# A decoder trunk on one core: decays' differences on VectorE, attention heads in token order, four weight loads moved behind the last operands

## The chip, the cores and the metric

The kernel runs on 1 core of a Trainium2 chip. The metric is device time in microseconds of one execution; the time before is the median of three runs. Engines: PE is TensorE (matrix products), DVE is VectorE, ACT is ScalarE, POOL is GpSimd, SP is SyncE, which here issues nearly all transfers. Each engine works through its own queue in the order in which the program put it there, and an instruction that waits holds everything behind it in that queue.

## The reference

Sequence 512, model width 1024, float32. Two layers, each a mixer and a feed-forward part with a residual; an RMS norm stands ahead of each and at the end.

```python
for i in range(2):
    h = rmsnorm(x, mix_norm_w[i])
    x = x + (dilated_attention_mixer(h) if i == 0 else ssd_mixer(h))
    x = x + conv_ffn(rmsnorm(x, ffn_norm_w[i]))
return rmsnorm(x, final_norm_w)
```

The attention has 8 heads of 128, each with three dilations (1, 4, 16) that a softmax joins. The second mixer is a chunked state-space scan; its part that the change touches is the decay matrix of each head and chunk of 128 tokens, with `a_cs` the running sum of the decay rates:

```python
seg  = a_cs[:, :, :, None] - a_cs[:, :, None, :]
lmat = exp(where(causal, seg, -inf))
y_diag = einsum("bcijgr,bcjgrp->bcigrp", cb[..., None] * lmat, xdt)
```

It has 32 heads of 64 in 8 groups, and each group is closed by a gated RMS norm of its own.

## The kernel before

Activations lie as 8 tiles of 128 features by 512 tokens. Every float32 operand of a large product is split in a high and a low part (`xh`/`xl` for activations, `hi`/`lo` for weights), and `mm3` makes a product of three matmuls of 512 columns. A weight unit of 128x1024 comes by a transfer into `raw` (4 buffers), a cast on ACT (`hi`, L125) and a difference on DVE (`lo`, L126; `load_unit`). Results land in PSUM banks: `mm_bank` gives three in a ring, so a product can start only when the engine that reads the bank's last result but two has done so. That reader is a DVE instruction: `us` (L694, in `ssm_tile`: `usxs`, `usb`, `usc`, `usz`) for a projection of the state-space mixer, the sum into the residual `xr` (L872) for its output rows `wso`.

*Order.* PE's order is written out by hand (`manual_schedule`). That of DVE, ACT, POOL and SP is set by the scheduler that records the program, from its own estimates; `queued(name)` and `issue_after` hold an instruction behind a named one in that order.

*Attention.* `attend(h)` works in a token order by residue of 4. Its last step adds the bank `po` (rows in blocks, then residue) to a copy of `pg` into `o`, and splits `o` into `oh`, `ol`. After the last head the output product `wo` is added into `xr` (L551), where the tokens are brought back into natural order by a strided access on both SBUF operands; `prep` then splits `xr[m]` into `xh[m]`, `xl[m]` (L200, L201) and sums its squares.

*Norm and projection.* `norm_and_project` runs the first three projections behind a norm while the last `xh`/`xl` come in: k = 0 to 6 of two of them, then k = 7. The mean goes PE (`ss`), DVE (`ms`), POOL (`rcol`), PE (`rb`), ACT (`rbc`). It is used twice: ahead of the first feed-forward (units `u0_0` to `u0_2`) and ahead of the state-space mixer (`xs00`, `wdt`, `b0`).

*State-space mixer.* `project_group(g)` makes x0, b, c, x1, z0, z1 of group g, `scan_group(g)` the scan. While PE projects group g + 1, the scan of group g goes: `decays` (four tiles `lm` and two `ee`, read back from `rows` by transfers; differences and exponentials on ACT), `by_token` (`xdt` on DVE from the bank `px`, `xdd` on POOL, `btok` on ACT), `cb` (DVE), `states` (PE `pst`), `lm` times `cb` (POOL), `products` (PE `py`, `pf`), `outputs` (DVE `yt`, ACT squares `gsq`), the sum of the two squares (DVE L840), the mean and the norm. The differences of the next group (L768, 16 instructions of 128x128) are held behind the second square of the group before; `latest["square"]` names it.

Of the kernel before, what the change touches and what calls it, by code (L numbers as in the profile page):

```python
# [22 lines left out]
DIL = 4  # L23
# [28 lines left out]
def trunk(ctx: ExitStack, tc: tile.TileContext, A, out):  # L52
    nc = tc.nc
    V, SC, G, T = nc.vector, nc.scalar, nc.gpsimd, nc.tensor
# [12 lines left out]
    def mm_bank(name):  # L67
        return ps.tile([P, 512], F32, tag="mm", name=name, bufs=3)
# [7 lines left out]
    def t2(name, tag, bufs, pool=k2, dtype=F32):  # L76
        return pool.tile([P, 512], dtype, tag=tag, name=name, bufs=bufs)
# [32 lines left out]
    def col(c):  # L110
        return par[:, c : c + 1]
# [21 lines left out]
    def long_product(dst, w, x, first, last):  # L133
        T.matmul(in_turns(dst), w, in_turns(x), start=first, stop=last)  # L134

    def mm3(dst, hi, lo, at, rh, rl, first, last):
        w_h = hi[:, at * P : (at + 1) * P]
        w_l = lo[:, at * P : (at + 1) * P]
        long_product(dst, w_h, rh, first, False)
        long_product(dst, w_h, rl, False, False)  # L140
        long_product(dst, w_l, rh, False, last)

    early = {}

    def project(src, name, low=V):
        if name in early:
            return early.pop(name)
        hi, lo = load_unit(src, name, low=low)
        t = mm_bank(name)
        for k in range(KD):  # L150
            mm3(t, hi, lo, k, xh[k], xl[k], k == 0, k == KD - 1)
        return t

    def norm_and_project(ssum, srcs):

        units = [(load_steps() if name == "wdt" else load_unit(src, name), mm_bank(name), name) for src, name in srcs]

        def part(i, ks):
            (hi, lo), t, name = units[i]
            for k in ks:  # L160
                if name == "wdt":
                    steps_products(t, hi, k)
                else:
                    mm3(t, hi, lo, k, xh[k], xl[k], k == 0, k == KD - 1)

        with tc.manual_schedule(engines={mybir.EngineType.PE}):
            part(0, range(KD - 1))
            part(1, range(KD - 1))
            part(0, [KD - 1])
            part(1, [KD - 1])  # L170
            inv_rms(ssum, D, rcol)
            part(2, range(5))
            p = along_free(rcol, "rb")
            SC.copy(rbc, p)
            part(2, range(5, KD))
        for _, t, name in units:
            early[name] = t

    def load_steps():

        raw = wr.tile([P, 1024], F32, tag="raw", name="raw_wdt")[:, : KD * NSH]
        both = wh.tile([P, 1088], F32R, tag="hi", name="hi_wdt")[:, : 2 * KD * NSH]
        dma(raw, A["wdt"])
        raw3, both4 = raw.rearrange("p (k h) -> p k h", k=KD), both.rearrange("p (k b h) -> p k b h", k=KD, b=2)
        SC.copy(both4[:, :, 0], raw3)
        V.tensor_tensor(both4[:, :, 1], raw3, both4[:, :, 0].bitcast(F32), op=ALU.subtract)
        return both, None

    def steps_products(dst, both, k):
        w = both[:, k * 2 * NSH : (k + 1) * 2 * NSH]  # L190
        long_product(dst[0 : 2 * NSH, :], w, xh[k], k == 0, False)
        long_product(dst[0 : 2 * NSH, :], w, xl[k], False, k == KD - 1)


    def prep(k, src, c_w, ssum):
        split(k, src, c_w)
        square(k, src, ssum)

    def split(k, src, c_w):
        SC.activation(xh[k], src, AF.Copy, scale=col(c_w + k))  # L200
        V.scalar_tensor_tensor(  # L201
            xl[k], src, col(c_w + k), xh[k].bitcast(F32), op0=ALU.mult, op1=ALU.subtract
        )

    def square(k, src, ssum, add=G):
        if k == 0:
# [94 lines left out]
    ssum = t2("ssum", "ssum", 2)  # L301
# [45 lines left out]
    def in_blocks(ap):  # L347

        return ap.rearrange("p (n r l) -> p r n l", n=4, r=DIL)

    def by_residue(ap):
        return ap.rearrange("p (r n l) -> p r n l", n=4, r=DIL)

# [28 lines left out]
    scale = HD ** -0.5  # L382
    oh, ol = [], []

    def attend(h):
# [89 lines left out]
        po, pg = aux_bank(f"po{h}"), aux_bank(f"pg{h}")  # L475
# [5 lines left out]
        values(2)  # L481
        values(3)
        o = t2(f"o{h}", "o", 1, s3)
        SC.copy(in_blocks(o), by_residue(pg))
        V.tensor_tensor(o, o, po, op=ALU.add)
        o_h, o_l = high_low(f"o{h}")
        SC.copy(o_h, o)
        V.tensor_tensor(o_l, o, o_h.bitcast(F32), op=ALU.subtract)
# [49 lines left out]
    xr = [lp.tile([P, S], F32, tag=f"xr{k}", name=f"xr{k}") for k in range(KD)]  # L538
    for k in range(KD):
        dma(xr[k], A["xt"][k])  # L540

    def natural(ap):
        return ap.rearrange("p (n l r) -> p n r l", n=4, r=DIL)

    ssum = t2("ssum1", "ssum", 2)
    for m in range(KD):
        if m not in wo_held:
            wo_first(m)
        hi, lo, p = wo_held[m]
        mm3(p, hi, lo, NH - 1, oh[-1], ol[-1], False, True)  # L550
        V.tensor_tensor(  # L551
            natural(xr[m]), natural(xr[m]), p.rearrange("p (n r l) -> p n r l", n=4, r=DIL),
            op=ALU.add
        )
        prep(m, xr[m], C_FFN, ssum)


# [45 lines left out]
            with tc.manual_schedule(engines={mybir.EngineType.PE}):  # L603
                down(f"wd{layer}{part}", load, range(KD), lambda c: (gh[c], gl[c]), cn, add, late=True)

    def up_first(layer):
        return [(A["wup"][layer * 44 + i], f"u{layer}_{i}") for i in range(3)]

    norm_and_project(ssum, up_first(0))
    ssum_a = t2("ssum2", "ssum", 2)  # L610
    ffn(0, lambda m: prep(m, xr[m], C_MIX + KD, ssum_a))
    norm_and_project(ssum_a, [(A["win"][0], "xs00"), (A["wdt"], "wdt"), (A["win"][2], "b0")])


    def b3(ap, n):
# [8 lines left out]
    dtt, adt, acs, dec, cdec = (cst(n) for n in ("dtt", "adt", "acs", "dec", "cdec"))  # L624
# [60 lines left out]
    latest = {}  # L685
# [33 lines left out]
    def scan_group(g, d, ys):  # L719
# [34 lines left out]
        def decays():  # L754

            for x in range(2):
                ee.append(t2("ee", "ee", 2, lp))
                for hp in range(2):
                    h, half = heads[x].start + hp, slice(hp * 64, (hp + 1) * 64)
                    t = t2("lm", "lm", 4, lp)  # L760
                    dma(t, rows[h : h + 1, :].to_broadcast([P, S]))
                    dma(ee[x][half, P:512], rows[h : h + 1, P:512].to_broadcast([64, S - P]))
                    lm.append(t)
            with queued("square"):
                for i, t in enumerate(lm):
                    for c in range(NCH):
                        cs, at = slice(c * P, (c + 1) * P), c * NSH + heads[0].start + i
                        SC.activation(t[:, cs], t[:, cs], AF.Relu, bias=acs[:, at : at + 1], scale=-1.0)  # L768
            with queued("gate"):
                for x in range(2):  # L770
                    SC.activation(ee[x][:, P:512], ee[x][:, P:512], AF.Exp)
                for t in lm:
                    latest["decay"] = SC.activation(t, t, AF.Exp, scale=-1.0)

        def products(x):

# [22 lines left out]
        def outputs(x, py, pf):  # L799
            yt = t2("yt", "yt", 2, lp)  # L800
            V.tensor_tensor(ee[x][:, P:512], ee[x][:, P:512], pf[:, P:512], op=ALU.mult)
            V.scalar_tensor_tensor(
                yt, xs[x], col(C_DSK + 2 * g + x), py, op0=ALU.mult, op1=ALU.add
            )
            V.tensor_tensor(yt[:, P:512], yt[:, P:512], ee[x][:, P:512], op=ALU.add)
            V.tensor_tensor(yt, yt, d[f"z{x}"], op=ALU.mult)
            sq = t2("gsq", "sq", 2)
            latest["square"] = SC.activation(sq, yt, AF.Square)
            return yt, sq

        decays()
# [10 lines left out]
        for c in range(NCH):  # L822
            cs = slice(c * P, (c + 1) * P)
# [13 lines left out]
        banks = [f() for f in carried]  # L837
        yield
        (y0, sq0), (y1, sq1) = (outputs(x, *b) for x, b in enumerate(banks))
        V.tensor_tensor(sq0, sq0, sq1, op=ALU.add)  # L840
        yield
        rg = sm.tile([P, 4], F32, tag="rg", name="rg")
        latest["mean"] = inv_rms(sq0, 2 * P, rg, bank=side_bank)
# [325 lines left out]
```

## Time and profile before

| | |
|---|---|
| median of the runs | 1653.52 us (1652.71 to 1653.53, 3 runs) |
| profiled execution | 1652.15 us, span 1650.4 us |
| mean granted clock of TensorE | 0.999 |
| busy: PE, DVE, ACT, POOL | 1633.2, 1039.9, 695.3, 456.9 us |
| stretches | attention to about 515 us, feed-forward to 858, state-space mixer to 1285, feed-forward to the end |

Busy time of PE counts overlapping matmuls once, so what matters is where it waits, and what ends the wait. In the chain that ended last, PE has 86%, DVE 6%, ACT 4%.

### The profile page before, as it was taken

The page shows a single profiled execution, that of the slowest core. Times are in us where ns is not written, and L with a number is a line of the kernel's source. Part 1 is how long each engine was busy: PE and PEld are TensorE (multiplying, and loading weights), DVE is VectorE, ACT ScalarE, POOL GpSimd, SP SyncE. Part 2 cuts the span into 40 slices and gives each one's busy share as a digit, 9 for nine tenths or more (in the row PEclk, how much of TensorE's full clock was granted, in tenths as well). Part 3 has the DMA queues.
Part 4 walks back from the last instruction along what each step waited for, and adds up shares of the span by engine and source line. Part 5 has one row for each costly group of instructions (what it writes and reads, how often), then busy time and mean ns, then how long its engine had stood idle before and what let it go on. Part 6 is the DMA issues. An engine that isn't in the chain of part 4 may idle for free.

```text
span 1650.4 us, 21521 instructions
## 1 busy us (share of the span) xinstructions
PE 1633.2 (99%) x8236; PEld 1396.8 (85%) x8236; DVE 1039.9 (63%) x1672; ACT 695.3 (42%) x1115; POOL 456.9 (28%) x294
## 2 busy tenths in 40 slices
PE   9999999999999999999999999999999999999998
PEld 8888888888888888888888887888878888888888
DVE  6366555366648755755656677766777684574565
ACT  5233332333345433432445745555562552343345
POOL 0443443044503310220232222332331341121022
PEclk9999999999999999999999999999999999999999
DMA  7322222222224323323233333233432332332323
GB/s 255 103 79 75 80 88 89 90 77 90 77 80 138 101 87 106 102 90 115 74 109 121 105 114 104 74 122 112 138 102 74 101 104 89 115 102 90 104 76 128
DMA packets 54391, 168.32 MB, mean 102 GB/s; under 512 B 6353, under 2 KB 9809, under 8 KB 54289
## 3 DMA queue, kind: packets, MB, share of 16 engines
q1 hardware_dynamic: 53456, 166.15, 30.4%
q8 instruction: 65, 1.06, 0.3%
q10 hardware_dynamic: 832, 0.79, 0.1%
q14 instruction: 38, 0.30, 0.1%
HBM read 164.76 MB, written 2.16 MB: 101 GB/s over the span
## 4 chain that ended last, share of the span: by engine, by line
PE 86%; DVE 6%; ACT 4%; issue 2%; DMA 2%; POOL 0%; DVEq 0%; POOLq 0%; ACTq 0%; SPq 0%
PE u L134 28%; PE qk L134 15%; PE wd L134 12%; PE v L134 8%; PE wso L134 3%; PE xs L134 3%; PE z L134 3%; PE b L134 2%; PE c L134 2%; PE wo L134 2%; PE wz L134 1%; ACT lm L768 1%; DVE axs L561 1%; PE pp L448 1%; PE pg L461 1%
## 5 line engine op out<-in xcount | busy, mean ns | idle before, releaser
L134 PE MATMUL u<-xh,lo_u 128*128 128x512 f32 x704 | 269.0, 382 | 0.0
L134 PE MATMUL u<-xh,hi_u 128*128 128x512 f32 x704 | 268.7, 382 | 0.0
L134 PE MATMUL u<-xl,hi_u 128*128 128x512 f32 x704 | 266.4, 378 | 0.3 <-DVE xl L201 0.3
L583 POOL TENSOR_TENSOR au<-au,au 128x512 f32<-128x512 f32 x43 | 56.9, 1322 | 423.8 <-DVE au L561 397.3
L561 DVE SCALAR_TENSOR_TENSOR au<-usu,par,au 128x510 f32<-128x510 f32 (+1 forms) x176 | 160.8, 918 | 6.2 <-ACT au L559 1.3
L363 POOL TENSOR_TENSOR rotqk<-rotqk,sr 32x512 f32<-32x512 f32 x48 | 91.9, 1915 | 256.3 <-DVE rotqk L362 208.9
L125 ACT CAST hi_u<-raw_u 128x1024 fp32r<-128x1024 f32 x88 | 91.2, 1044 | 169.9 <-PE u L134 97.1
L134 PEld LDWEIGHTS u<-xl,hi_u 128*128 128x128 f32 x704 | 131.7, 187 | 25.2 <-DVE xl L201 0.7
L134 PEld LDWEIGHTS u<-xh,lo_u 128*128 128x128 f32 x704 | 131.7, 187 | 23.9
L134 PEld LDWEIGHTS u<-xh,hi_u 128*128 128x128 f32 x704 | 131.7, 187 | 21.5
L134 PE MATMUL qk<-xh,hi_qk 128*128 128x512 f32 x384 | 148.8, 388 | 0.0
L134 PE MATMUL qk<-xh,lo_qk 128*128 128x512 f32 x384 | 147.1, 383 | 0.0
L134 PE MATMUL qk<-xl,hi_qk 128*128 128x512 f32 x384 | 147.0, 383 | 0.0
L126 DVE TENSOR_TENSOR lo_u<-raw_u,hi_u 128x1024 fp32r<-128x1024 f32 x88 | 111.1, 1268 | 25.9 <-ACT hi_u L125 25.9
L576 DVE TENSOR_TENSOR usu<-u,rbc 128x512 f32<-128x512 f32 x88 | 60.5, 690 | 103.1 <-PE u L134 93.8
L596 DVE TENSOR_TENSOR xr<-xr,wd 128x512 f32<-128x512 f32 x40 | 27.2, 687 | 117.2 <-PE wd L134 117.2
L125 ACT CAST hi_qk<-raw_qk 128x1024 fp32r<-128x1024 f32 x48 | 50.2, 1046 | 99.6 <-PE v L134 49.8
L125 ACT CAST hi_wd<-raw_wd 128x1024 fp32r<-128x1024 f32 (+1 forms) x56 | 52.4, 952 | 90.2 <-PE wd L134 55.9
L359 DVE TENSOR_TENSOR qk<-qk,cr 128x512 f32<-128x512 f32 x48 | 33.0, 687 | 90.5 <-PE qk L134 90.3
L134 PEld LDWEIGHTS qk<-xh,lo_qk 128*128 128x128 f32 x384 | 71.9, 187 | 13.0
L134 PEld LDWEIGHTS qk<-xl,hi_qk 128*128 128x128 f32 x384 | 72.0, 187 | 12.4
L134 PEld LDWEIGHTS qk<-xh,hi_qk 128*128 128x128 f32 x384 | 71.9, 187 | 11.7
(641 smaller groups left out, 3909.1 us busy)
## 6 DMA issues: line engine op xcount, KB each, us to landing
raw_u<-in_wup SPq DMA_DIRECT2D x88, 512.0 KB, 3.2
raw_qk<-in_wqk SPq DMA_DIRECT2D x48, 512.0 KB, 3.2
raw_wd<-in_wdn SPq DMA_DIRECT2D x32, 512.0 KB, 3.2
raw_wd<-in_wdn SPq DMA_DIRECT2D x24, 384.0 KB, 3.0
raw_xs<-in_win SPq DMA_DIRECT2D x16, 512.0 KB, 3.2
raw_z<-in_win SPq DMA_DIRECT2D x16, 512.0 KB, 4.0
lm<-rows SPq DMA_DIRECT2D x32, 256.0 KB, 5.5
raw_wso<-in_wso SPq DMA_DIRECT2D x16, 512.0 KB, 3.3
```

The lines of the kernel that those rows point to most:

```text
L125: SC.copy(hi[:, s], raw[:, s])
L126: low.tensor_tensor(lo[:, s], raw[:, s], hi.bitcast(F32)[:, s], op=ALU.subtract)
L134: T.matmul(in_turns(dst), w, in_turns(x), start=first, stop=last)
L359: V.tensor_tensor(at(t), of(p), of(cr), op=ALU.mult)
L363: G.tensor_tensor(rot[R, :], rot[R, :], sr[R, :], op=ALU.mult)
L448: T.transpose(pp[:, b * P : (b + 1) * P], pr[:, b * P : (b + 1) * P], ident)
L461: T.matmul(pg[:, ii], vt[g, half][i][:, es], pts[i][:, (g + 1) * P : (g + 2) * P], start=g == 1, stop=g == 2,)
L561: V.scalar_tensor_tensor(dst[:, j:], src[:, : S - j], col(c_w + taps - 1 - j), dst[:, j:], op0=ALU.mult, op1=ALU.add,)
L576: V.tensor_tensor(us, p, rbc, op=ALU.mult)
L583: by.tensor_tensor(ab[1], ab[0], ab[1], op=ALU.mult)
L596: V.tensor_tensor(xr[m], xr[m], p, op=ALU.add)
L768: SC.activation(t[:, cs], t[:, cs], AF.Relu, bias=acs[:, at : at + 1], scale=-1.0)
```

## The change

Four edits. The 16 differences of each group are computed on DVE (subtract and a minimum with 0 in place of a Relu of the negated difference; the exponential loses its sign), and they are held behind the sum of the two squares instead of the second square. `o` is written in natural token order: ACT's copy and DVE's sum carry the strides, and the sums into `xr` become plain. `norm_and_project` takes two further units (`u0_3`, `u0_4`; `c0`, `xs01`) whose loads are issued behind the last `xh` and `xl`; `project` then finds them in `loaded`. `square` of the outputs is otherwise unchanged.

```diff
+    loaded = {}
     early = {}
     def project(src, name, low=V):
         if name in early:
             return early.pop(name)
-        hi, lo = load_unit(src, name, low=low)
+        hi, lo = loaded.pop(name) if name in loaded else load_unit(src, name, low=low)
...
-    def norm_and_project(ssum, srcs):
+    def norm_and_project(ssum, srcs, more):
...
+        with tc.issue_after(last_split[0].ins), tc.issue_after(last_split[1].ins):
+            for src, name in more:
+                loaded[name] = load_unit(src, name)
...
-        SC.copy(in_blocks(o), by_residue(pg))
-        V.tensor_tensor(o, o, po, op=ALU.add)
+        SC.copy(o.rearrange("p (n l r) -> p r n l", n=4, r=DIL), by_residue(pg))
+        V.tensor_tensor(natural(o), natural(o), po.rearrange("p (n r l) -> p n r l", n=4, r=DIL), op=ALU.add)
...
-        V.tensor_tensor(
-            natural(xr[m]), natural(xr[m]), p.rearrange("p (n r l) -> p n r l", n=4, r=DIL),
-            op=ALU.add
-        )
+        V.tensor_tensor(xr[m], xr[m], p, op=ALU.add)
...
-    norm_and_project(ssum, up_first(0))
+    norm_and_project(ssum, ups(0, range(3)), ups(0, (3, 4)))
...
-    norm_and_project(ssum_a, [(A["win"][0], "xs00"), (A["wdt"], "wdt"), (A["win"][2], "b0")])
+    norm_and_project(ssum_a, [(A["win"][0], "xs00"), (A["wdt"], "wdt"), (A["win"][2], "b0")], [(A["win"][3], "c0"), (A["win"][1], "xs01")])
...
-                        SC.activation(t[:, cs], t[:, cs], AF.Relu, bias=acs[:, at : at + 1], scale=-1.0)
+                        V.tensor_scalar(t[:, cs], t[:, cs], acs[:, at : at + 1], 0.0, op0=ALU.subtract, op1=ALU.min)
...
-                    latest["decay"] = SC.activation(t, t, AF.Exp, scale=-1.0)
+                    latest["decay"] = SC.activation(t, t, AF.Exp)
...
-            latest["square"] = SC.activation(sq, yt, AF.Square)
+            SC.activation(sq, yt, AF.Square)
...
-        V.tensor_tensor(sq0, sq0, sq1, op=ALU.add)
+        latest["square"] = V.tensor_tensor(sq0, sq0, sq1, op=ALU.add)
```

What stands in the queues: PE's order and that of SP's transfers are the same before and after. On DVE, at the end of group 2, before (`usz` and `usxs` read the banks of the last z and of the x projected ahead, `xr` those of two `wso`):

```order
L806 TENSOR_TENSOR yt<-yt,usz_7725 128x512
L694 TENSOR_TENSOR usz_8195<-z_8170,rbc 128x512
L806 TENSOR_TENSOR yt<-yt,usz_7815 128x512
L126 TENSOR_TENSOR lo_c_8408<-raw_c_8406,hi_c_8407 128x1024
L840 TENSOR_TENSOR gsq<-gsq 128x512
L694 TENSOR_TENSOR usxs_8265<-xs_8240,rbc 128x512
L872 TENSOR_TENSOR xr_4046<-xr_4046,wso_8285 128x512
L126 TENSOR_TENSOR lo_xs_8486<-raw_xs_8484,hi_xs_8485 128x1024
```

and after:

```order
L813 TENSOR_TENSOR yt<-yt,usz_7725 128x512
L701 TENSOR_TENSOR usz_8195<-z_8170,rbc 128x512
L813 TENSOR_TENSOR yt<-yt,usz_7815 128x512
L126 TENSOR_TENSOR lo_c_8408<-raw_c_8406,hi_c_8407 128x1024
L847 TENSOR_TENSOR gsq<-gsq 128x512
L775 TENSOR_SCALAR lm<-lm,acs 128x128 x16
L701 TENSOR_TENSOR usxs_8265<-xs_8240,rbc 128x512
L126 TENSOR_TENSOR lo_xs_8486<-raw_xs_8484,hi_xs_8485 128x1024
L879 TENSOR_TENSOR xr_4046<-xr_4046,wso_8285 128x512
```

The sixteen differences (L775) stand ahead of `usxs`; `usz` stays ahead of them. At the end of group 3 on DVE, before:

```order
L806 TENSOR_TENSOR yt<-yt,usz_8195 128x512
L840 TENSOR_TENSOR gsq<-gsq 128x512
L694 TENSOR_TENSOR usz_8643<-z_8618,rbc 128x512
L126 TENSOR_TENSOR lo_c_8856<-raw_c_8854,hi_c_8855 128x1024
L694 TENSOR_TENSOR usxs_8713<-xs_8688,rbc 128x512
```

and after:

```order
L813 TENSOR_TENSOR yt<-yt,usz_8195 128x512
L847 TENSOR_TENSOR gsq<-gsq 128x512
L775 TENSOR_SCALAR lm<-lm,acs 128x128 x16
L701 TENSOR_TENSOR usz_8643<-z_8618,rbc 128x512
L126 TENSOR_TENSOR lo_c_8856<-raw_c_8854,hi_c_8855 128x1024
L701 TENSOR_TENSOR usxs_8713<-xs_8688,rbc 128x512
```

Here `usz` too has the sixteen ahead of it; groups 4 and 5 read alike. At the end of group 6 on DVE, before (the first two `xr` are sums of `wso` of groups 2 and 3, the later ones of group 4):

```order
L840 TENSOR_TENSOR gsq<-gsq 128x512
L872 TENSOR_TENSOR xr_4052<-xr_4052,wso_9976 128x512
L872 TENSOR_TENSOR xr_4053<-xr_4053,wso_9990 128x512
L730 TENSOR_TENSOR xdt<-px,dtt 128x512 x2
L826 TENSOR_TENSOR cb<-pc,tri 128x512
L228 TENSOR_SCALAR ms<-ss 128x4
L126 TENSOR_TENSOR lo_wso_10183<-raw_wso_10181,hi_wso_10182 128x1024
L872 TENSOR_TENSOR xr_4046<-xr_4046,wso_10044 128x512
L126 TENSOR_TENSOR lo_wso_10189<-raw_wso_10187,hi_wso_10188 128x1024
```

and after:

```order
L847 TENSOR_TENSOR gsq<-gsq 128x512
L775 TENSOR_SCALAR lm<-lm,acs 128x128 x16
L879 TENSOR_TENSOR xr_4052<-xr_4052,wso_9976 128x512
L126 TENSOR_TENSOR lo_wso_10183<-raw_wso_10181,hi_wso_10182 128x1024
L879 TENSOR_TENSOR xr_4053<-xr_4053,wso_9990 128x512
L737 TENSOR_TENSOR xdt<-px,dtt 128x512 x2
L126 TENSOR_TENSOR lo_wso_10189<-raw_wso_10187,hi_wso_10188 128x1024
L833 TENSOR_TENSOR cb<-pc,tri 128x512
L237 TENSOR_SCALAR ms<-ss 128x4
L879 TENSOR_TENSOR xr_4046<-xr_4046,wso_10044 128x512
```

The sum into `xr_4046` now stands behind the sixteen and behind both `lo_wso`. On ACT the differences are gone and the rest keeps its order in most groups; on POOL, at the end of group 1, one `lo_z` moves ahead of `xdd`.

## Rows read from the trace of the kernel before

**Rows 1.** The page: busy time of PE, its share of the span and its instructions (with the other engines), and the clock granted to TensorE in 40 equal slices, in tenths of full speed.

```profile
PE 1633.2 (99%) x8236; PEld 1396.8 (85%) x8236; DVE 1039.9 (63%) x1672; ACT 695.3 (42%) x1115; POOL 456.9 (28%) x294
...
PEclk9999999999999999999999999999999999999999
```

**Rows 2.** Who PE's matmuls waited for: us in total, times, longest us.

```profile
PE wso L134 <- DVE xr L872: 3.3, 1, 3.3
PE pst L741 <- ACT btok L819: 2.9, 1, 2.9
PE wso L134 <- DVE usz L694: 1.3, 2, 0.8
...
PE xs L134 <- DVE xl L201: 0.6, 1, 0.6
...
PE b L134 <- DVE usxs L694: 0.3, 1, 0.3
PE u L134 <- DVE xl L201: 0.3, 1, 0.3
```

**Rows 3.** Groups of instructions by line and shape: count, busy us, mean ns of one, idle us of the engine just before them and what ended it. First ACT, then DVE.

```profile
L768 ACT ACTIVATE lm<-lm,acs 128x128 f32<-128x128 f32 x128 | 38.5, 388 | 0.4 <-DMA lm<-rows 0.4
...
L359 DVE TENSOR_TENSOR qk<-qk,cr 128x512 f32<-128x512 f32 x48 | 33.0, 687 | 90.5 <-PE qk L134 90.3
...
L551 DVE TENSOR_TENSOR xr<-xr,wo 128x512 f32<-128x512 f32 x8 | 9.4, 1189 | 7.2 <-PE wo L134 7.2
...
L485 DVE TENSOR_TENSOR o<-o,po 128x512 f32<-128x512 f32 x8 | 5.4, 680 | 5.8 <-ACT o L484 5.8
...
L445 DVE TENSOR_SCALAR pr<-pr,join 128x128 f32<-128x128 f32 x8 | 2.3, 287 | 0.3
```

**Rows 4.** DVE in order of time in one attention head: start us, us, engine, line, operation, and how many in a row.

```profile
161.85 2.12 DVE L445 TENSOR_SCALAR pr<-pr,join 128x128 f32<-128x128 f32 x8
```

**Rows 5.** In order of time around the first `u`: PE, with the wait in brackets and what ended it, then DVE.

```profile
510.44 0.38 PE L134 MATMUL u<-xh,lo_u 128*128 128x512 f32 x1
510.66 0.38 PE L134 MATMUL u<-xh,hi_u 128*128 128x512 f32 x1
511.37 0.49 PE L134 MATMUL u<-xl,hi_u 128*128 128x512 f32 x1 [0.33 <-DVE xl L201]
...
510.57 0.74 DVE L201 SCALAR_TENSOR_TENSOR xl<-xr,par,xh 128x512 fp32r<-128x512 f32 x1
```

**Rows 6.** In order of time around the first `xs`: DVE, then PE.

```profile
859.77 1.22 DVE L126 TENSOR_TENSOR lo_xs<-raw_xs,hi_xs 128x1024 fp32r<-128x1024 f32 x1
...
862.74 0.49 PE L134 MATMUL xs<-xl,hi_xs 128*128 128x512 f32 x1 [0.57 <-DVE xl L201]
...
875.72 0.49 PE L134 MATMUL c<-xh,hi_c 128*128 128x512 f32 x1
```

**Rows 7.** In order of time behind the ends of group 0 (first row) and group 1 (the others): DVE, POOL, ACT, PE.

```profile
951.96 6.27 DVE L561 SCALAR_TENSOR_TENSOR axs<-usxs,par,axs 128x511 f32<-128x511 f32 x3 [5.96 <-ACT axs L559]
...
991.00 0.69 DVE L840 TENSOR_TENSOR gsq<-gsq 128x512 f32<-128x512 f32 x1 [2.79 <-ACT gsq L808]
...
992.21 1.27 DVE L730 TENSOR_TENSOR xdt<-px,dtt 128x512 f32<-128x512 f32 x2
...
998.80 5.37 DVE L561 SCALAR_TENSOR_TENSOR axs<-usxs,par,axs 128x511 f32<-128x511 f32 x3 [4.71 <-ACT axs L559]
...
992.97 1.63 POOL L731 TENSOR_TENSOR xdd<-xdt,dec 128x384 f32<-128x384 f32 x2 [7.45 <-DVE xdt L730]
...
998.67 0.46 ACT L819 COPY btok<-pb 128x384 f32<-128x384 f32 x1
...
999.27 1.58 PE L741 MATMUL pst<-xdd,btok 128*128 128x128 f32 x12 [2.88 <-ACT btok L819]
```

**Rows 8.** In order of time behind the end of group 2: DVE, then PE.

```profile
1035.01 0.69 DVE L840 TENSOR_TENSOR gsq<-gsq 128x512 f32<-128x512 f32 x1 [2.40 <-ACT gsq L808]
1035.62 0.68 DVE L694 TENSOR_TENSOR usxs<-xs,rbc 128x512 f32<-128x512 f32 x1
...
1041.57 1.23 DVE L126 TENSOR_TENSOR lo_xs<-raw_xs,hi_xs 128x1024 fp32r<-128x1024 f32 x1 [4.67 <-ACT hi_xs L125]
...
1036.69 0.47 PE L134 MATMUL b<-xh,hi_b 128*128 128x512 f32 x1
```

**Rows 9.** In order of time behind the end of group 3: DVE, then PE.

```profile
1081.57 0.69 DVE L840 TENSOR_TENSOR gsq<-gsq 128x512 f32<-128x512 f32 x1 [0.70 <-ACT gsq L808]
1082.18 0.68 DVE L694 TENSOR_TENSOR usz<-z,rbc 128x512 f32<-128x512 f32 x1
...
1082.92 0.50 PE L134 MATMUL wso<-y00h,hi_wso 128*128 128x512 f32 x1 [0.49 <-DVE usz L694]
```

**Rows 10.** In order of time behind the end of group 6: POOL, DVE, then PE.

```profile
1223.52 2.37 POOL L126 TENSOR_TENSOR lo_z<-raw_z,hi_z 128x1024 fp32r<-128x1024 f32 x1 [20.09 <-ACT hi_z L125]
...
1224.00 2.44 DVE L840 TENSOR_TENSOR gsq<-gsq 128x512 f32<-128x512 f32 x1 [0.97 <-ACT gsq L808]
...
1232.90 1.45 DVE L126 TENSOR_TENSOR lo_wso<-raw_wso,hi_wso 128x1024 fp32r<-128x1024 f32 x1 [3.40 <-ACT hi_wso L125]
1234.28 0.67 DVE L872 TENSOR_TENSOR xr<-xr,wso 128x512 f32<-128x512 f32 x1
...
1235.01 0.48 PE L134 MATMUL wso<-y40h,hi_wso 128*128 128x512 f32 x1 [3.28 <-DVE xr L872]
```

More of the change, by code (lines that the diff above doesn't have):

```diff
@@ L197, in prep @@
         square(k, src, ssum)
+    last_split = []
     def split(k, src, c_w):
-        SC.activation(xh[k], src, AF.Copy, scale=col(c_w + k))
-        V.scalar_tensor_tensor(
-            xl[k], src, col(c_w + k), xh[k].bitcast(F32), op0=ALU.mult, op1=ALU.subtract
-        )
+        last_split[:] = [
+            SC.activation(xh[k], src, AF.Copy, scale=col(c_w + k)),
+            V.scalar_tensor_tensor(
+                xl[k], src, col(c_w + k), xh[k].bitcast(F32), op0=ALU.mult, op1=ALU.subtract
+            ),
+        ]
     def square(k, src, ssum, add=G):
@@ L349, in in_blocks, with natural @@
         return ap.rearrange("p (n r l) -> p r n l", n=4, r=DIL)
+    def natural(ap):
+        return ap.rearrange("p (n l r) -> p n r l", n=4, r=DIL)
     def by_residue(ap):
@@ L540, in trunk @@
         dma(xr[k], A["xt"][k])
-    def natural(ap):
-        return ap.rearrange("p (n l r) -> p n r l", n=4, r=DIL)
     ssum = t2("ssum1", "ssum", 2)
@@ L550, in trunk @@
         mm3(p, hi, lo, NH - 1, oh[-1], ol[-1], False, True)
-        V.tensor_tensor(
-            natural(xr[m]), natural(xr[m]), p.rearrange("p (n r l) -> p n r l", n=4, r=DIL),
-            op=ALU.add
-        )
+        V.tensor_tensor(xr[m], xr[m], p, op=ALU.add)
         prep(m, xr[m], C_FFN, ssum)
@@ L604, in ffn, with ups @@
                 down(f"wd{layer}{part}", load, range(KD), lambda c: (gh[c], gl[c]), cn, add, late=True)
-    def up_first(layer):
-        return [(A["wup"][layer * 44 + i], f"u{layer}_{i}") for i in range(3)]
-    norm_and_project(ssum, up_first(0))
+    def ups(layer, some):
+        return [(A["wup"][layer * 44 + i], f"u{layer}_{i}") for i in some]
+    norm_and_project(ssum, ups(0, range(3)), ups(0, (3, 4)))
     ssum_a = t2("ssum2", "ssum", 2)
     ffn(0, lambda m: prep(m, xr[m], C_MIX + KD, ssum_a))
-    norm_and_project(ssum_a, [(A["win"][0], "xs00"), (A["wdt"], "wdt"), (A["win"][2], "b0")])
+    norm_and_project(ssum_a, [(A["win"][0], "xs00"), (A["wdt"], "wdt"), (A["win"][2], "b0")], [(A["win"][3], "c0"), (A["win"][1], "xs01")])
     def b3(ap, n):
```

## The prediction

> **What bounds the kernel now.** The page comes first: TensorE (PE) is busy for 99% of the span, and its granted clock is full in every slice [rows 1]. So the time is PE's queue of products, whose order the change keeps, plus the places where that queue stands still. The second view is therefore PE's own waits [rows 2]. They are few, and the two longest, 3.3 and 2.9 us, lie in the state-space mixer: one for a sum into `xr` on DVE, one for a copy `btok` on ACT. A wait costs a little more than its row says: products start 0.22 apart, but the one at 511.37 starts 0.71 after the one before, so a wait of 0.33 costs 0.49, and I add 0.16 to each [rows 5]. The third view is the order of time around each wait [rows 5 to 10]; there the reader should look at which queue, ACT's or DVE's, holds the instruction that PE names, and behind what.
>
> T(g) is the start of the sum `gsq<-gsq` on DVE that ends group g of the mixer; the sixteen new differences of the next group stand right behind it. T(1) is 991.00, T(2) 1035.01, T(3) 1081.57, T(6) 1224.00 [rows 7 to 10].
>
> **Price of the new work.** No row shows VectorE's subtract-and-min of 128x128 with a column operand. The nearest is a multiply of the same shape by a column. Eight in a row, one of 128 columns and seven of 256, take 2.12 [rows 4]; a mean of 287 ns stands for one of 128 [rows 3]. With 0.274 for each of the seven, the first leaves room of 0.20 for the next. Bounds are 0.14 (half of 0.274, if columns were all that counts) and 0.287. I take 0.20, the same shape: 16 cost **3.25** of DVE in each group (2.2 to 4.6). ACT loses 128 differences, 38.5 us in all [rows 3], 4.8 in each group.
>
> **Heads and weights (134 to 515).** Eight sums into `xr` fall from 1189 to the 680 ns of a sum without strides, and the eight sums of `o` rise by as much; ACT's copy of `o` may also slow [rows 3]. DVE idles for 90 us before L359, waiting for PE, and for 7.2 behind the last head's sum, before L551 [rows 3], so these 8 times 0.5 us are hidden; without that cover they would cost up to 4. Of what the sums into `xr` give back only what ends PE's wait counts. `xl` at 510.57 ends it [rows 5]; one of the moved `lo_u` (1.2 us) and a strided sum stood ahead of it. Both go: **-0.5**. At 862.74 PE waits 0.57 for an `xl` behind two `lo` of 1.22, which are moved: **-0.7** [rows 6]. Each of the four moved loads brings its cast on ACT and its difference on DVE along; the transfers keep their order on SyncE's queue, and a raw buffer comes free some 3 us later there. `c` is first read at 875.72, 13 us on [rows 6], which hides this; the instruction for the mean, queued behind them on DVE, needs PE's `ss`, which comes later still. Bounds: 0 and -1.5.
>
> **The mixer's hand-overs.** After each T(g), ACT now runs 4.8 us of differences, and DVE then idles for something queued behind them on ACT: 5.96 in group 1, 4.71 in group 2, 4.67 in group 3 [rows 7, 8]. Into these holes go 3.25. If nothing else holds, DVE's chain gains 5.96 - 3.25 = 2.7 in the first and 4.71 - 3.25 = 1.5 in the second. So T(1) comes 2.7 earlier and T(2) about **4** (1.5 if data or casts hold it up, 5.5 if the first group, whose differences also leave ACT, adds its share).
> - *T(1).* PE's 2.88 for `btok`, which ACT copies at 998.67 behind the differences, goes. What is late next is `xdt` on DVE, behind the sixteen: 992.21 - 2.7 + 3.25 = 992.8; GpSimd's two `xdd` start 0.76 after it and take 1.63: 995.2. PE comes at 996.2 (999.27 - 2.88 - 0.16). **-3.0** [rows 7]. Without the lead `xdd` ends at 997.9, and 1.4 remain.
> - *T(2).* The longer of the two waits for `usz`, 0.8 + 0.16 [rows 2], goes: `usz` stays ahead of the sixteen. **-0.95.** But `usxs` frees the bank of the next product `b`, and now stands behind them. It ends at 1031.0 + 0.6 + 3.25 + 0.7 = 1035.55, while PE, 3.95 earlier, would start `b` at 1036.69 - 3.95 = 1032.75 [rows 8]. That is a new wait: **+2.8** (5.3 if the lead is 1.5; 1.3 if it is 5.5).
> - *T(3).* Here `usz` itself moves behind the sixteen, and PE takes its bank at 1082.92 [rows 9]. The hole of 4.67 adds 1.4 to the lead, 5.4: `usz` ends at 1076.2 + 4.55 = 1080.7. PE, ready 0.65 ahead of that start and 1.15 earlier by now, comes at 1081.1. So the 0.5 + 0.16 go, and so do the 0.3 + 0.16 for `usxs` at `b` [rows 2], as `lo_c` ahead of it no longer waits for a cast behind the differences. **-1.1.** Later hand-overs show no such wait.
> - *T(6).* PE waits 3.28 for a sum into `xr` (1234.28 on DVE) behind a `lo_wso` that ACT's queue holds for 3.40 [rows 10]. The cast comes earlier now, but more stands ahead of that sum: the `gsq` sum 0.6, the sixteen 3.25, two `xr` 1.2, two `lo` 2.4, two `xdt` 1.2, `cb` and the mean 0.7, itself 0.7, together 10.05. GpSimd's `lo_z` of 2.37 runs beside the start: the `gsq` sum takes 2.44 there and 0.69 in group 1 [rows 7, 10], so I add 1.75. T(6) may lead PE by 2.5, an estimate below T(2)'s 4, as PE's own data bound DVE by then: 1221.5 + 11.8 = 1233.3, against 1234.95. **-1.65** (-3.4 without `lo_z`, +0.7 without lead).
>
> The Trainium skill (SBUF — State Buffer, section Who interferes with whom) says that a `tensor_scalar` in a two-port mode and a GpSimd instruction shut each other out for the whole instruction, as does a DVE instruction with two inputs in SBUF beside a GpSimd one that reads it. The stretched sum at 1224.00 agrees for the second kind; for the first no row here does, and by the rule the sixteen too are held wherever `lo_z` meets them, which is the third rival.
>
> **Sum.** -0.5 - 0.7 - 3.0 - 0.95 + 2.8 - 1.1 - 1.65 = **-5.1**. The profiled execution took 1652.15, 1.75 beyond its span of 1650.4, so 1647.05. The median of the runs shown, 1653.52, is 1.37 above it, and I forecast **1648.4**, 0.31% faster. 0.2%, 3.3 us, is about what a measurement of this kernel can tell from no change.
>
> **Rivals.**
> - *The sixteen cost what they free (chance 0.20).* With a lead of 1.5 at T(2), `b` starts at 1038.05, 1.35 later than now, whatever was won before it; then -1.2, -1.1 and +0.7 make -0.25: 1653.3. With none at all `usz` at T(3) ends 3.25 late: -1.2 + 3.25 - 0.45 + 0.7 = +2.3: 1655.8. For it: after T(3) ACT's own step on `usz`, ahead of its exponentials, waits for DVE's, behind the sixteen. Against: the holes exceed 3.25.
> - *Slower: DVE sets the pace (0.11).* At 0.287 the sixteen cost 4.6, the holes leave no lead, and one stretched instruction of 1.75 falls into the chain. `usxs` at T(2) then ends 4.6 + 1.75 = 6.35 late, `b` starts 6.0 late, `usz` at T(3) adds 0.9: -1.2 + 6.9 - 0.45 + 0.7 = +6: 1659.5. It decides from about 0.25 each on. For it: both banks are taken within 0.4 us of being freed [rows 8, 9].
> - *The shared port (0.10).* GpSimd now has a `lo_z` of 2.37 ahead of `xdd` at T(1). If the sixteen are held by it, `xdd` ends 2.4 later, at 997.6 against 996.2, and T(2) loses 1.0 of its lead: -2.7, 1650.8.
> - *Every wait goes (0.07).* A lead of 7 at T(2) and no `lo_z` at T(6): -5.1 - 2.8 - 1.75: 1643.9.
>
> My own case has 0.52, by itself 1645 to 1651. **Faster 0.57, same 0.31, slower 0.12**, with a tenth of my case and most of the port's in the middle. Leaving out the slower rival and the lower half of the last gives **1643.5 to 1656**.
>
> **What would show it.** Right: 128 `TENSOR_SCALAR` on `lm`, 0.20 apart; no PE wait for `btok`, none for `xl`; a new one of 2 to 3 us of `b` for `usxs` at T(2); none for `usz` at T(3). Wrong: a wait over 2 us for `usz` at T(3), or for `xdd` at T(1), means there is no lead; differences 0.28 apart or more mean the price was wrong; PE waits of over 14 us in all mean a slower kernel.

## The result, and the profile after

The changed kernel takes **1657.42 us** (median of 20 executions, 1654.93 to 1658.79) against 1653.89 for the kernel before (20 executions): ratio 1.0019, 95% interval 1.0013 to 1.0026, so 0.2% slower. The forecast was 1648.4, 0.3% faster, with a range of 1643.5 to 1656.0.

The profiled execution took 1654.93, the shortest of the twenty, with a span of 1653.2, against 1650.4 before. The page of it, as [rows 1]:

```profile
PE 1633.6 (99%) x8236; PEld 1398.1 (85%) x8236; DVE 1070.1 (65%) x1800; ACT 661.8 (40%) x985; POOL 452.0 (27%) x294
```

VectorE took on 30 us and ScalarE lost 33.5; PE has the work that it had. Who PE's matmuls waited for (us in total, times, longest), as [rows 2]:

```profile
PE pst L748 <- POOL xdd L738: 3.0, 1, 3.0
PE b L134 <- DVE usxs L701: 2.6, 1, 2.6
PE wso L134 <- DVE xr L879: 2.3, 1, 2.3
PE pf L798 <- DVE prev L755: 2.1, 2, 1.2
...
PE wso L134 <- DVE usz L701: 0.8, 1, 0.8
PE px L735 <- DVE yt L809: 0.6, 1, 0.6
```

Both waits for `xl` are gone, and `btok` is gone as a releaser. In its place `xdd` stands with about the same length, and three lines are new or longer: `b` for `usxs`, `pf` for `prev` (twice), `px` for `yt`. PE's order is the same in both kernels, so the start of the same product in both traces says what each place gave or took:

| product, us before | after minus before | step there |
|---|---|---|
| `u` 506.7, `ss` 518.1, `wdt` 863.3 | -0.59, -1.38, -2.09 | start and heads -0.6, `xl` -0.8, `xl` -0.7 |
| `pf` 970.5, `prg` 971.9, `px` 984.3 | -0.83, -0.54, +0.08 | `prev` +1.5, `yt` +0.6 |
| `ss` 1000.7, `pf` 1014.3 | +0.32, +1.21 | `xdd` for `btok` +0.2, `prev` +0.9 |
| `b` 1036.7, `wso` 1042.1 | +3.97, +5.62 | `usxs` +2.8, slow products +1.65 |
| `px` 1085.8, `b` 1089.2 | +4.76, +4.27 | `usz` -0.9, `usxs` -0.5 |
| `ss` 1226.5, `z` 1236.8 | +3.64, +2.80 | `gsq` -0.6, `xr` -0.8 |

The last number is the whole difference of the spans. Up to 863 and behind 1042 the changed kernel gained 4.9 in all; the stretch between, the first three hand-overs of the mixer, lost 7.7.

**Hand-over T(0).** In order of time (start us, us, engine, line, operation, how many in a row, and in brackets the idle time ahead and what ended it): DVE, then POOL, then ACT.

```profile
939.63 0.69 DVE L847 TENSOR_TENSOR gsq<-gsq 128x512 f32<-128x512 f32 x1 [0.70 <-ACT gsq L815]
940.24 5.17 DVE L775 TENSOR_SCALAR lm<-lm,acs 128x128 f32<-128x128 f32 x15
945.32 0.68 DVE L701 TENSOR_TENSOR usz<-z,rbc 128x512 f32<-128x512 f32 x1
...
952.69 5.61 DVE L568 SCALAR_TENSOR_TENSOR axs<-usxs,par,axs 128x511 f32<-128x511 f32 x3 [4.10 <-ACT axs L566]
...
940.61 2.35 POOL L126 TENSOR_TENSOR lo_z<-raw_z,hi_z 128x1024 fp32r<-128x1024 f32 x1 [23.86 <-ACT hi_z L125]
...
946.04 0.63 ACT L704 ACTIVATE usz<-usz 128x512 f32<-128x512 f32 x1 [5.50 <-DVE usz L701]
...
948.82 2.18 ACT L780 ACTIVATE lm<-lm 128x512 f32<-128x512 f32 x4
```

ACT no longer spends 5 us on differences; it waits as long, 5.50 for `usz`, which stands on DVE behind fifteen of the sixteen. Behind it come the table load and all exponentials, and only then the step of `axs` for which DVE stands idle another 4.10 (5.96 in [rows 7]). And the sixteen do not take 3.25 but 5.4 (5.96 from the first start to the last end, with `usz` among them): all are 0.28 long but one, which takes 2.42 beside `lo_z` of 2.35. From the `gsq` sum to `axs` it is 13.1, where it was 12.1 before; the sum of the kernel before:

```profile
939.82 0.69 DVE L840 TENSOR_TENSOR gsq<-gsq 128x512 f32<-128x512 f32 x1 [0.70 <-ACT gsq L808]
```

**Hand-over T(1).** DVE, POOL, PE:

```profile
991.25 0.69 DVE L847 TENSOR_TENSOR gsq<-gsq 128x512 f32<-128x512 f32 x1 [2.98 <-ACT gsq L815]
991.86 5.43 DVE L775 TENSOR_SCALAR lm<-lm,acs 128x128 f32<-128x128 f32 x16
997.21 0.68 DVE L701 TENSOR_TENSOR usxs<-xs,rbc 128x512 f32<-128x512 f32 x1
997.81 1.27 DVE L737 TENSOR_TENSOR xdt<-px,dtt 128x512 f32<-128x512 f32 x2
...
994.47 2.53 POOL L126 TENSOR_TENSOR lo_z<-raw_z,hi_z 128x1024 fp32r<-128x1024 f32 x1 [8.88 <-ACT hi_z L125]
998.56 1.62 POOL L738 TENSOR_TENSOR xdd<-xdt,dec 128x384 f32<-128x384 f32 x2 [1.56 <-DVE xdt L737]
...
999.44 1.73 PE L748 MATMUL pst<-xdd,btok 128*128 128x128 f32 x12 [2.97 <-POOL xdd L738]
```

T(1) comes at 991.25, where it came at 991.00 before. Again there is a stretched block, 5.43, and what is late for PE is no longer ScalarE's copy but `xdt` and `xdd` behind the block.

**Hand-over T(2).** DVE, then PE, then a table by stretch (stretch, its length, busy time and instructions of PE, PEld, DVE, ACT and POOL, granted clock of TensorE, DMA share, GB/s):

```profile
1036.79 3.22 DVE L775 TENSOR_SCALAR lm<-lm,acs 128x128 f32<-128x128 f32 x16
1039.93 0.68 DVE L701 TENSOR_TENSOR usxs<-xs,rbc 128x512 f32<-128x512 f32 x1
...
1040.66 0.49 PE L134 MATMUL b<-xh,hi_b 128*128 128x512 f32 x1 [2.63 <-DVE usxs L701]
...
1042.90 0.63 PE L134 MATMUL b<-xh,lo_b 128*128 128x512 f32 x1
1043.33 0.63 PE L134 MATMUL b<-xh,hi_b 128*128 128x512 f32 x1
...
1042.00:1046.00 4.00, 4.00 (x13) 3.12 (x12) 3.96 (x7) 0.88 (x1) 0.21 (x1) 0.57 0.39 131
```

With no GpSimd work beside them the sixteen take 3.22; 3.25 was forecast. PE waits 2.63 for the `usxs` behind them, and 1.4 us after it goes on, its products start 0.43 apart and not 0.22: the granted clock fell to the lower of its two levels (1.2 of 2.4 GHz) for some 3.4 us.

### The profile page after: what moved, and what is told of

The parts are those of the page before. It is cut to its first block, busy times and chain, and to the rows that moved or that the text cites. A ratio compares the mean times of both kernels' runs of the same rounds, so it can differ in the third digit from the quotient of the medians.

```text
span 1653.2 us, 21510 instructions
## 1 busy us (share of the span) xinstructions
PE 1633.6 (99%) x8236; PEld 1398.1 (85%) x8236; DVE 1070.1 (65%) x1800; ACT 661.8 (40%) x985; POOL 452.0 (27%) x294
## 4 chain that ended last, share of the span: by engine, by line
PE 88%; DVE 6%; ACT 2%; DMA 1%; issue 1%; POOL 0%; DVEq 0%; SPq 0%; POOLq 0%; ACTq 0%
PE u L134 28%; PE qk L134 15%; PE wd L134 12%; PE v L134 8%; PE wso L134 4%; PE xs L134 3%; PE z L134 3%; PE wo L134 3%; PE b L134 2%; PE c L134 2%; DVE lm L775 2%; PE wz L134 1%; DVE axs L568 1%; PE pp L461 1%; PE pg L474 1%
## 5 line engine op out<-in xcount | busy, mean ns | idle before, releaser
L134 PEld LDWEIGHTS qk<-xh,lo_qk 128*128 128x128 f32 x384 | 71.9, 187 | 13.1
```

## The experiments

All times are medians beside runs of the kernel before on the same chip (1653.57, 1653.74 and 1653.88 in the three sessions); a ratio is to these, over all executions.

**1. Heads and loads alone.** In the changed kernel, with the hold back on the second square:

```diff
-V.tensor_scalar(t[:, cs], t[:, cs], acs[:, at : at + 1], 0.0, op0=ALU.subtract, op1=ALU.min)
+SC.activation(t[:, cs], t[:, cs], AF.Relu, bias=acs[:, at : at + 1], scale=-1.0)
...
-latest["decay"] = SC.activation(t, t, AF.Exp)
+latest["decay"] = SC.activation(t, t, AF.Exp, scale=-1.0)
```

> The changed kernel with its differences given back to ScalarE (Relu, behind the second Square, as before); the heads' order and the moved loads stay. Theory: the traces of before and after stand 2.1 us apart in TensorE's queue at 861, ahead of the mixer, in favour of the changed kernel, and the loss begins with the sixteen: about 2.1 under the kernel before, 1651.8, with the waits for btok and xr of the kernel before back in the mixer. Rival 1, the loads or the heads' order do the harm later on: 1656 or more. Rival 2, the 2.1 are lost again in the mixer, since a wait there ends by ScalarE's own pace: 1653.9.

Measured: 1651.58, ratio 0.9992 (0.9983 to 1.0000). The theory's time. T(0) comes at 937.60, against 939.63 in the changed kernel, so the sixteen cost 2 us already in group 0. Of PE's waits of before, `xr` and `btok` are back:

```profile
937.60 0.69 DVE L847 TENSOR_TENSOR gsq<-gsq 128x512 f32<-128x512 f32 x1 [0.70 <-ACT gsq L815]
...
PE wso L134 <- DVE xr L879: 3.4, 1, 3.4
PE pst L748 <- ACT btok L826: 2.4, 1, 2.4
```

The short waits for `usz`, `usxs` and `gsq` do not show: in this execution the clock is low behind `btok`, PE falls back there, and what it waited for before is now in time.

**2. Differences alone.** In the kernel before:

```diff
-SC.activation(t[:, cs], t[:, cs], AF.Relu, bias=acs[:, at : at + 1], scale=-1.0)
+V.tensor_scalar(t[:, cs], t[:, cs], acs[:, at : at + 1], 0.0, op0=ALU.subtract, op1=ALU.min)
...
-V.tensor_tensor(sq0, sq0, sq1, op=ALU.add)
+latest["square"] = V.tensor_tensor(sq0, sq0, sq1, op=ALU.add)
```

> The kernel before with the differences alone moved to VectorE behind the squares' sum. Theory: everything that is lost comes from them, and the 2.1 us won ahead of the mixer are missing: the measured 1657.4 plus 2.1, 1659.5. Rival, the parts work on each other (only a mixer that starts 2.1 earlier loses): 1655 to 1657.

Measured: 1658.90, ratio 1.0033 (1.0021 to 1.0045). The parts add up: the whole loss comes from the differences, and the other two edits are worth about 2 (1653.57 less the first's 1651.58). Its profile has the same new waits (`xdd` 2.8, `usxs` 2.7, `prev` 2.5).

**3. Behind `usz`.**

```diff
-            V.tensor_tensor(us, p, rbc, op=ALU.mult)
+            scaled = V.tensor_tensor(us, p, rbc, op=ALU.mult)
         if c_conv is None:
+            latest["scaled"] = scaled
...
-            with queued("square"):
+            with queued("scaled"), queued("square"):
```

> The changed kernel with the sixteen of a group queued behind VectorE's multiply that makes usz of the same hand-over (in the changed kernel it stands behind fifteen of them at T(0) and behind all at T(3)). Theory, the lead fails since ScalarE's exponentials wait for its own step on usz, which waits for VectorE's behind the sixteen: the table load and two exponentials of ee, 2.2 us, go ahead of the sixteen's end, the waits of 1.4 for prev, 0.3 and 0.8 in group 1 go; the wait of b for usxs at T(2) stays: 1657.4 - 2.2 = 1655.2. Rival, VectorE's sum of work alone sets the pace, wherever the sixteen stand: 1657.4.

Measured: 1653.22, ratio 0.9995 (0.9986 to 1.0004), which does not meet the changed kernel's interval. ACT, then DVE, at T(0), and last the sum at T(1):

```profile
940.81 0.63 ACT L705 ACTIVATE usz<-usz 128x512 f32<-128x512 f32 x1 [0.42 <-DVE usz L701]
...
940.69 5.18 DVE L776 TENSOR_SCALAR lm<-lm,acs 128x128 f32<-128x128 f32 x16
...
948.22 2.27 DVE L568 SCALAR_TENSOR_TENSOR axs<-usxs,par,axs 128x511 f32<-128x511 f32 x1 [0.56 <-ACT axs L566]
...
987.33 0.69 DVE L848 TENSOR_TENSOR gsq<-gsq 128x512 f32<-128x512 f32 x1 [2.80 <-ACT gsq L816]
```

ACT's wait falls from 5.50 to 0.42, and from the `gsq` sum to `axs` it is 8.7 us (the sum starts at 939.48), against 13.1 in the changed kernel and 12.1 before. That is twice the gain that I expected: two of the four exponentials of `lm` (943.61 to 944.97) now also run beside the sixteen. T(1) comes at 987.33, 3.9 earlier. The wait for `usxs` at T(2) stays at 2.6. In PE's queue 3.9 are won up to there and 1.2 lost again, as the low clock lasts 6.8 us and not 3.4; so the spans differ by 2.7, and the medians by 4.2.

**4. Behind `usxs`.** The third's hold, with the handle set by every tile's multiply, and the next `xs` written ahead of the differences:

```diff
-                    if i == 2 and j == 0 and g < NSG - 1:
+                    if i == 2 and j == (1 if g < NSG - 3 else 0) and g < NSG - 1:
```

> The changed kernel with the tile behind usz (the next group's first xs) written ahead of the differences, and the sixteen queued behind its multiply usxs; ScalarE's own first step of axs then also stands ahead of the exponentials. Theory: the 2.8 us wait of b for usxs at T(2) goes, and with it the 1.6 us of half clock behind it; with the 2.2 of usz that is 6.6: 1650.8. Rival 1, the wait comes back at xdt or at the products on lm, behind later exponentials: 1655 to 1657. Rival 2, the half clock does not hang on this wait: it shows elsewhere, 1652.5.

Measured: **1646.28**, ratio 0.9951 (0.9939 to 0.9964), 4.5 under the theory's 1650.8. In PE's queue the gain on the changed kernel is 6.5 ahead of T(2) and 4.3 there, and it stays at 10.8. At T(2) DVE now has

```profile
1030.35 0.68 DVE L701 TENSOR_TENSOR usxs<-xs,rbc 128x512 f32<-128x512 f32 x1
1030.95 3.23 DVE L775 TENSOR_SCALAR lm<-lm,acs 128x128 f32<-128x128 f32 x16
```

and `b` starts at 1031.49 without a wait; the granted clock is 1.00 from 1028 to 1045. The sixteen are not cheaper (the block at T(0) takes 6.6 here); they stand where they keep less waiting.

**5. `lo_z` off GpSimd, twice.**

```diff
-        p = project(A["win"][i], name, V if c_conv is not None else G)
+        p = project(A["win"][i], name, V if c_conv is not None or name in ("z20", "z31") else G)
```

> The changed kernel with the differences lo_z of two weight units (z20 and z31) on VectorE in place of GpSimd: those are the two that run beside the sixteen at T(0) and T(1) in its trace, where one of the sixteen takes 2.4 us. Theory, the two engines shut each other out: with no GpSimd work beside them the sixteen take 3.2 us in both places, not 6.0 and 5.4; VectorE pays 1.2 for each lo, so the chain gains about 1.5 and 1.0, of the measured 1657.4 some 2 go: 1655.4. Rival, the long one of the sixteen is late for another reason (its row's load): it stays at 2.4, and with 1.2 more in each place 1659.

Measured: 1652.92, ratio 0.9995 (0.9987 to 1.0004). The differences of both hand-overs (min, median, max ns), first in the changed kernel, then here:

```profile
L775 DVE TENSOR_SCALAR lm<-lm,acs x32: 271/280/2477, 940.2 to 997.0; 128x128 f32<-128x128 f32 x32
```
```profile
L775 DVE TENSOR_SCALAR lm<-lm,acs x32: 277/282/284, 941.1 to 993.4; 128x128 f32<-128x128 f32 x32
```

The long ones are gone, although DVE has 2.4 us more to do. The Trainium skill (SBUF — State Buffer, section Who interferes with whom) says that a `tensor_scalar` in a two-port mode and a GpSimd instruction shut each other out for the whole instruction; the two fences agree with it, though no row tells in which mode the sixteen run. From T(0) to T(1) it is 49.3, against 51.6 in the changed kernel and 51.2 before. The spans of the two profiles differ by 2.1, as expected, but the medians by 4.5. The other 2.4 stay open: most executions of the changed kernel have a mean granted clock of 0.995 or 0.996, its profiled one 0.998, and no trace shows one of the others.

**6. Behind `usxs` at T(2) alone.** As the fourth, with `1 if g == 2 else 0`, and the hold `queued("scaled")` for the sixteen of that place only.

> The changed kernel with the edit of the fourth experiment at T(2) alone: there the sixteen stand behind usxs, everywhere else they stay where they are. Theory, the wait of b for usxs (2.8) and the half clock behind it (1.6 in the profile) both hang on this place: 1657.4 - 4.4 = 1653.0, with no product of b at 0.43. Rival, the half clock belongs to the waits of the whole stretch (3.1 for xdd at T(1) stays): it shows elsewhere, 1654.6. The remaining 6 to 7 us of the fourth experiment would then come from groups 1 and 2.

Measured: 1654.54, ratio 1.0003 (0.9995 to 1.0012): the rival's time, and for its reason in part. `b` does not wait, and there PE's queue gains 4.4 on the changed kernel. But of this 2.3 are given back one hand-over later, where `usz` still stands behind the sixteen:

```profile
PE wso L134 <- DVE usz L701: 2.6, 2, 2.0
```

and the low clock shows at T(1), behind the wait of 2.8 for `xdd`, where the changed kernel's own profile has the full clock behind a wait of 2.97:

```profile
1000.00:1003.00 3.00, 2.51 (x11) 2.51 (x12) 2.96 (x4) 0.00 (x0) 3.00 (x4) 0.56 0.21 86
```

**7. Behind `usxs`, and five `lo_z` off GpSimd.** The fourth, with `("z11", "z20", "z21", "z31", "z71")` in the line of the fifth.

> The kernel of the fourth experiment with five units' lo_z (z11, z20, z21, z31, z71) on VectorE: all those that run beside sixteen differences or beside the squares' sum at T(6). Theory, exclusion costs the chain more than the differences: at T(6) the squares' sum takes 0.69, not 2.44, and TensorE's wait of 2.4 for xr falls to about 1; at T(1) the 0.5 for xdd goes: 1646.3 - 1.9 = 1644.4. Rival, five times 1.2 of new work on VectorE eats it: 1646.3 or more.

Measured: **1641.83**, ratio 0.9931 (0.9918 to 0.9943), 2.6 under the theory. All blocks of sixteen but the first group's take 3.2, T(0) comes at 937.47, the time of the first experiment (939.56 in the fourth): the 2 us of group 0 go with `lo_z` beside the first group's differences. The sum at T(6) takes 0.69, and the view of PE's waits lists one in the mixer:

```profile
PE wso L134 <- DVE xr L879: 1.9, 1, 1.9
```

**8. The last group's sixteen later.** The fourth, with the differences as a function of their own, which the last group calls behind the step that makes `cb`; a sum into `xr` now also sets the handle that they are held behind:

```diff
         yield
+        if g == NSG - 1:
+            differences()
         for x in range(2):
             states(x)
```

> The kernel of the fourth experiment with the last group's sixteen (those at T(6)) written one step later, so that they stand on VectorE behind the sums into xr which free TensorE's banks there. Theory, the sixteen ahead of these sums are what TensorE waits for (2.4 and 0.3 in the trace): 1646.3 - 2.7 = 1643.6. Rival, the exponentials of the last group then come too late for its products on lm, and a wait of 2 to 4 us stands there: 1646 to 1648.

Measured: 1643.58, ratio 0.9938 (0.9924 to 0.9951): the theory's time, but in part by luck. The wait of 2.3 for `xr` at T(6) goes, and one for a later `xr` comes 12 us on:

```profile
1239.38 0.49 PE L134 MATMUL wso<-y40h,hi_wso 128*128 128x512 f32 x1 [1.46 <-DVE xr L886]
```

The spans of the fourth and the eighth differ by 0.8 only. The medians differ by 2.7, but they are of unlike executions: three of the fourth's five had a mean granted clock of 0.998, four of the eighth's five 0.999. Those with 0.999 took 1644.4 and 1643.7 on average.

**9. Seventh and eighth together.**

> The seventh and the eighth experiments together: the sixteen behind usxs, five units' lo_z on VectorE, and the last group's sixteen one step later. Theory, the two act on different places: at T(6) the eighth took away 2.7 us for xr and gave 1.6 back later, so 1641.8 - 1.1 = 1640.7, or down to 1639.1 if with VectorE ahead the sum into xr that waits there is early enough. Rival, with lo_z off GpSimd the wait at T(6) was short already: 1641.8.

Measured: 1641.76, ratio 0.9927 (0.9915 to 0.9940): the seventh's time, but not for the rival's reason. The first wait did go, from 1.94 at 1224.63 to nothing, and `z` behind it starts 2.0 earlier. It comes back 13 us on, as the sixteen now stand ahead of a later sum into `xr` on DVE:

```profile
1237.22 0.49 PE L134 MATMUL wso<-y40h,hi_wso 128*128 128x512 f32 x1 [1.46 <-DVE xr L886]
```

**10. ScalarE's differences with the same five `lo_z` on VectorE.** The first, with the line of the seventh.

> The first experiment (differences on ScalarE, heads' order and moved loads kept) with the same five units' lo_z on VectorE as the seventh. It parts the gain of the seventh into what the differences' engine gives and what lo_z gives by itself. Theory, ScalarE's 4.8 us in each hand-over still set T(1) and T(2), and lo_z met no difference there: 1651.6 less at most 1.2 for the squares' sum at T(6): 1650.4, so that the differences on VectorE, well placed, are worth over 8. Rival, lo_z on GpSimd was the real brake all along: 1645.

Measured: 1649.60, ratio 0.9976 (0.9966 to 0.9986), near the theory. So of the 10 us between the first and the seventh, `lo_z` by itself gives 2, and the differences on VectorE, well placed, 8. The 8 hold the new place of `xs` too; what that gives with the differences on ScalarE was not tried. `btok` and `usz` are still waited for, and `xr` more than ever:

```profile
PE wso L134 <- DVE xr L879: 4.1, 1, 4.1
PE wso L134 <- DVE usz L701: 1.1, 2, 0.7
...
PE pst L748 <- ACT btok L826: 1.0, 1, 1.0
```

**11 and 12. Heads alone, loads alone.** Each in the kernel before:

```diff
-V.tensor_tensor(o, o, po, op=ALU.add)
+V.tensor_tensor(natural(o), natural(o), po.rearrange("p (n r l) -> p n r l", n=4, r=DIL), op=ALU.add)
...
-    norm_and_project(ssum, up_first(0))
+    norm_and_project(ssum, ups(0, range(3)), ups(0, (3, 4)))
```

> The kernel before with the heads' rows in token order alone. Theory: the sum into xr that ends TensorE's wait at 511 takes 0.68 in place of 1.19, so of its 0.6 some 0.5 go, and nothing else moves: 0.5 under the kernel before in TensorE's queue, within the noise of the time. Rival, the strided copies and sums of o come late for TensorE: waits of 0.5 behind each head.

> The kernel before with the moved loads alone. Theory: the wait of 0.8 at 862 for xl goes and that of 0.6 at 511 goes or falls, since a difference of 1.2 no longer stands ahead of the last xl: 0.7 to 1.4 under the kernel before in TensorE's queue. Rival, the loads come late: c waits at 875, or u at 530.

Measured: 1652.90, ratio 0.9996 (0.9986 to 1.0006), and 1652.61, ratio 0.9994 (0.9984 to 1.0004): neither can be told from no change by its time. PE's queue tells more. With heads alone the wait for `xl` at 511 is gone (-0.79) and the one at 862 stays; with loads alone the first is halved and the second is gone (-0.70):

```profile
PE xs L134 <- DVE xl L201: 0.6, 1, 0.6
```
```profile
PE u L134 <- DVE xl L209: 0.2, 1, 0.2
```

## Why the prediction was wrong

**Right.** The price: 3.22 measured for sixteen, undisturbed, and 3.25 forecast. The two waits for `xl`: -1.49 for -1.2. Heads and loads are hidden, as the first experiment shows.

**Right in size, not for the reason forecast.** `b` for `usxs` at T(2): +2.77 for +2.8. The wait hangs on the difference of DVE's and PE's leads, which the forecast had at 4 and 3.95; both were late by 1.2 instead, and the difference is again near nothing. T(3): -1.35 for -1.1. There `usz` ends at 1083.8, not at 1080.7, and the waits go because PE comes 5 us later than before, where the forecast had it 1.15 earlier. T(6): -1.47 for -1.65, but only -0.84 of it where PE waits for `xr` (3.28 before, 2.27 after). The other -0.63 is a wait that the forecast did not price, and it too goes as PE is late; in the kernel before:

```profile
PE ss L223 <- DVE gsq L840: 0.4, 1, 0.4
```

One bound was slightly off: without a lead T(6) gives 1224.0 + 11.8 - 1234.95 = +0.85, not +0.7, which adds 0.15 to the three sums of the rivals that use it.

**Wrong: the lead.** The step that failed is "Into these holes go 3.25. If nothing else holds, DVE's chain gains 5.96 - 3.25 = 2.7". T(1) was to come 2.7 earlier and came 0.25 later, though PE began the mixer 2.1 earlier. Something else held, and the rivals name it in a half sentence: ScalarE's own step on `usz`, ahead of its exponentials, waits for DVE's, behind the sixteen. I looked for it after T(3), where `usz` stands behind them, and overlooked that at T(0) it stands behind fifteen. The hole in front of `axs` was not free: it is the time that ScalarE takes for `usz`, the table load and the exponentials, which now start only when VectorE has made `usz`. The third experiment changes the hold alone, and T(1) comes 3.9 earlier. The second hold is `lo_z`: I gave the shared port 0.10 and 1650.8, for T(1) alone. It struck at T(1), where `xdd` ends at 1000.2 for the forecast 995.2 (3.0 of it the missing lead, 2.2 the stretch); at T(0), where the fifth experiment shows its share; and in group 0, where it cost 2 us, while the forecast's upper bound counted on a gain there.

In the ledger of the profiles: T(0), which I had priced at nothing, +2.2 (`prev`, `yt`); T(1), +0.2 for -3.0, and +0.9 for `prev` behind it; T(2), where the wait for `usz` stayed, +0.95; the low clock, +1.65; all else -1.0. That is 7.9 from the forecast -5.1 to the measured +2.8. The remaining 1.1 lies between the profiled execution and the median: 2.5 us, where I took over the 1.37 of the kernel before. Where it comes from no trace shows.

**No rival came true as it stood.** "The sixteen cost what they free" has the nearest time, 1655.8 for no lead at all, 1.6 off, and the right hold, ScalarE's step on `usz`. But it put that hold after T(3), with `usz` 3.25 late for PE, and there PE does not wait. "DVE sets the pace" is 2.1 off with 1659.5, and the chain behind T(0) did get longer, 13.1 for 12.1. But its price was wrong (0.20, not 0.287), and its point of decision, 0.25 each, was reached on average only by the stretch, 0.33 at T(0) and 0.34 at T(1). That VectorE's work alone is not the bound is shown by the seventh experiment: there it is busy for 1071.0 us, against 1070.1 in the changed kernel, and the kernel takes 1641.83.

**Of the signs** I had named, the one for a kernel without a lead, a wait over 2 us for `xdd` at T(1), is there with 2.97. But the signs of my own case are there too (the stretched differences aside), so they did not tell it from the others. And the sign of a slower kernel, PE waits of over 14 us in all, is not: they come to 12.5 (10.4 before), and the time of the low clock is no wait.

## What to carry to other kernels

A hole in an engine's timeline is room for new work only if what ends it does not itself wait, one engine further, for something that the new work is put ahead of: follow the releaser back twice. When a block moves to another engine, its place in that queue is worth more than its cost: here the changed kernel was 0.2% slower with the sixteen behind the squares' sum, 0.5% faster with them behind the two multiplies that free banks, and 0.7% faster with the colliding GpSimd work moved as well. And look at which engine's instruction runs beside the block, not only at the block's length.

## What the runs showed of the hardware

- A VectorE subtract-and-min of 128x128 that met a GpSimd subtraction of 128x1024 took about that one's time: 2.42 and 2.48 us beside 2.35 and 2.53, in place of 0.28. Undisturbed, sixteen in a row take 3.22, a start every 0.20.
- PE's granted clock fell to the lower level at some waits of 2.2 to 4.1 us, for 3 to 7 us, and not at others just as long. The kernel before waits 2.88 for `btok` and 3.28 for `xr` and stays at full clock behind both; with heads alone it waits 2.88 and 3.29 at the same places and falls behind both (0.50 from 1000 to 1006, 0.55 from 1236 to 1239). What decides is open. Of 68 executions of the kernel before, 57 had a mean granted clock of 0.996 or 0.997 and took 1653.9 on average, 11 had 0.999 and took 1651.9; its profiled one was of the few. It is not a fixed price: of the first experiment's executions seven at 0.996 took 1651.6 on average, two at 0.997 took 1653.4 and two at 0.999 took 1651.5.
